# Sums of weight blocks made in DRAM during an earlier stage of the kernel

## The chip, the core and the metric

The kernel runs on one core of one Trainium2 chip. The engines of the core are named as in the profile: PE is TensorE with its matmuls, PEld its loading of weights, DVE is VectorE, ACT is ScalarE, POOL is GpSimd, SP is SyncE, which here only issues DMAs. The metric is the device time of one execution in microseconds. Before the change it is 2234.42 us, the median of 3 runs (2232.87 to 2238.69).

## What is computed

One transformer block in float32, on 512 tokens of width 2048. A normed input goes through one wide projection, and from it come a state-space mixer (SSD) and a sparse attention; their outputs are projected, and a gated feed-forward network follows.

```
u = rmsnorm(h, attn_norm_w)
z, xbc, dt_raw, q, kc, vc, ... = split(u @ w_in)
mixed = concat([ssd_mixer(z, xbc, ...), nsa_mixer(q, kc, vc, ...)])
h = h + mixed @ w_out
v = rmsnorm(h, ffn_norm_w)
h = h + (silu(v @ w_gate) * (v @ w_up)) @ w_down      # 2048 -> 5632 -> 2048
return rmsnorm(h, final_norm_w)
```

## The kernel before

**Precision.** Every float32 operand is split into a high half, a copy rounded to the type fp32r (made on ACT, line 121), and a low half, the difference (made on DVE, line 124). A product of two blocks is three matmuls: high by high, high by low, low by high.

**Order of the stages.** First the SSD part: the projection w_in in units of 128 columns, each of 16 blocks, with the mixer's own work woven in. Then attention and the output projection. Then the feed-forward network, first gate and up in 22 pairs (NP = 22), then down. A small scheduler (class Sched) holds generators for the woven work. Each block of a unit, that is each three matmuls, is one tick; a generator yields the number of ticks until it wants to go on. `ssd_core` (its tiles are `t`, `pf`, `xt` in the profile) and `compress` are such generators. In the SSD part and in attention the framework reorders the instructions of an engine by a timeline that it simulates; in the feed-forward part the order is the written one (`tc.manual_schedule()`, line 1937). A queue of instructions takes its waits in order on every engine.

**The feed-forward products.** They use a scheme of Strassen's kind. A 256 by 256 weight quarter has four blocks 11, 12, 21, 22, and instead of eight products of blocks it needs seven, M1 to M7. Three of the seven use sums: S1 = 21 + 22, S3 = 21 + 11, and on the way M6 takes S2 = 11 + S1, M3 takes S4 = 12 + 11 after 11 has become 11 + S1. (Signs are folded into how the blocks are stored and the tokens combined.) The other factors are seven forms of the tokens.

**Where sums are made before.** `quad` (line 1494) says for a group of n blocks how each operand comes about:

- gate and up pairs 0 to 20: S1 and S3 by DMA. SP loads 21, then POOL issues a DMA that adds 22 or 11 onto it (line 1292, `accum_op`).
- the last pair: S1 is added on POOL in place in SBUF, after loads of 21 and 22 (line 1275, in the profile line 130, the helper `add`).
- visits 0 to 5 of down: S1 and S3 are both added on POOL in SBUF (lines 1286 and 1275). Four loads a visit: 11, 12, 21, 22.
- visits from 6 on: S1 on POOL in place, S3 by a load of 21 and an accumulating DMA of 11.
- S2 and S4 always on DVE, in place, just before the high half is made (`form`, line 1308; line 130 in the profile, `Z<-Z` and the like).

**Visits of down.** The list `VISITS` gives 35 visits (j, n): output columns j (8 of them) by n of the 22 inner blocks; n is 2, 2, 3, 4, 5, 6, 6, 6 in the first eight and 4, 3, 3, 3, 5 in the last five. The first are small because the hidden activations (g_d, in DRAM, 1792 KB for an inner block) come back one by one through ACT's queue (`feed`, line 1742). The rows of H, one per j, are loaded from h_d by ACT's queue (line 1763). When the last visit of a column is through M6, `add_x` (lines 1809 to 1813) combines; after M5 `squares` (line 1774) takes squares on ACT for the last norm.

**Loads and places.** `advance` (line 1267) walks the list `loads` in order. For each entry it finds a free place in SBUF (zones Z, A, E; for down 38 places of 64 KB in Z, 8 in E, 6 in A), issues the load on SP's queue (line 1290), and with `plus` the accumulating DMA on POOL's queue (line 1292); an entry with `both` is added on POOL. Each `Blk` counts its reads and frees its place after the last.

Of the kernel before, what the change touches and what calls it, by code (L numbers as in the profile page):

```python
# [8 lines left out]
F32 = mybir.dt.float32  # L9
F32R = mybir.dt.float32r  # L10
AF = mybir.ActivationFunctionType
ALU = mybir.AluOpType
# [5 lines left out]
NP = NFF // 2  # L18
NJ = KD // 2
# [3 lines left out]
VISITS = [(0, 2), (1, 2), (2, 3), (3, 4), (4, 5), (5, 6), (6, 6), (7, 6), (1, 6), (0, 5), (2, 6), (3, 6), (4, 6), (5, 6),  # L23
          (6, 6), (7, 6), (0, 6), (1, 6), (2, 5), (3, 6), (4, 6), (6, 6), (5, 5), (7, 5), (0, 6), (1, 5), (2, 5), (3, 6),
          (5, 5), (4, 5), (6, 4), (0, 3), (1, 3), (2, 3), (7, 5)]
GRING = 8
G_US, MM_US, AHEAD_US = 7.0, 0.118, 5.0
KSUB = 4
EB = 5
LEAD = 3  # L30
NOA = 2


C_AN, C_FN, C_LN, C_SN, C_CW, C_CB, C_PE, C_W2 = 0, 16, 32, 48, 56, 104, 116, 148
# [9 lines left out]
M1, M2, M3, M4, M5, M6, M7 = range(1, 8)  # L44
# [67 lines left out]
def body(ctx, tc, xT, w_in, w_out, w_gate, w_up, w_down, w1k, w1v, cols, rows, kst, out):  # L112
    nc = tc.nc
    act, dve, pool, pe = nc.scalar, nc.vector, nc.gpsimd, nc.tensor
    sch = Sched()

    def f(ap):
        return ap.bitcast(F32)
# [7 lines left out]
    def mul(eng, o, a, b):  # L126
        eng.tensor_tensor(o, a, b, ALU.mult)  # L127
# [7 lines left out]
    dram = ctx.enter_context(tc.tile_pool(name="dram", bufs=1, space=bass.MemoryType.DRAM))  # L135
    def ps(tag, bufs):
        return psum.tile([128, 512], F32, tag=tag, name="ps_" + tag, bufs=bufs)
# [16 lines left out]
    gy_d = dram.tile([8, 2, 128, 512], F32, name="gy_d")  # L154
    y_d = dram.tile([4, 128, 512], F32, name="y_d")
    at_d = dram.tile([8, 128, 512], F32, name="at_d")
    h1_d = dram.tile([KD, 128, 512], F32, name="h1_d")
    h_d = dram.tile([NJ, 128, 4, 256], F32, name="h_d")
    g_d = dram.tile([NP, 4, 128, 896], F32, name="g_d")
    g8_d = dram.tile([NP // GRING, 7, 128, 512], F32, name="g8_d")  # L160

    pools = {}

    def open_pool(name, stack=None, **kw):
        es = ExitStack()
        pools[name] = (es, es.enter_context(tc.tile_pool(name=name, bufs=1, reuse_waits="tile", **kw)))
        return pools[name][1]
# [60 lines left out]
    def was_read(p):  # L228
        sch.flags.add(("evac", unit_of[id(p)]))
# [401 lines left out]
    def ev_kc(g):  # L631
        def ev(p):
            yield from sch.wait("r1")
            if g == 0:
                sp = pools["kcp"][1]
                R["kc2"] = sp.tile([128, 4, 256], F32, name="kc2")
                R["vc2"] = sp.tile([128, 4, 256], F32, name="vc2")
            for n, b in (("kc2", 0), ("vc2", 64)):
                for par in range(2):
                    mul(dve, R[n][par * 64:par * 64 + 64, g, :], p[b:b + 64, par::2], rrow[b:b + 64, par::2])  # L640
            was_read(p)
            if g == 3:
                sch.flags.add("kc")
        return ev

    def compress():
        yield from sch.wait("kc", "core")
# [529 lines left out]
    def ev_head(c):  # L1177
        def ev(p):
            P2["head", c] = p
            was_read(p)  # L1180
            yield 1
        return ev
# [4 lines left out]

    for c in range(NOA):
        units.append(Unit(w_out[c][:, 8:16, :], 8, ma_rhs, ev_head(c)))
# [191 lines left out]
    def pre_oa():  # L1381
# [29 lines left out]
        sch.add(stat_s())  # L1411
        for c in range(NOA):
            sch.add(head_oa(c))

    def head_oa(c):
        if c > 1:
            yield from sch.wait(("oa", c - 2))
        yield from ev_oa(c)(P2.pop(("head", c)))

    def stat_s():  # L1420
        yield 4
        yield from rms_stats(rrow, D, P2["srow"], "s", keep=True, gap=2)
# [55 lines left out]
    def oa_psum(c):  # L1478
        def get():
            if c >= NOA + 2:  # L1480
                sch.run_until(("oa", c - 2 - NOA))
            p = ps("gstgst"[(c // 2 + 0) % 3], 2)
            return p, p
        return get

    for c in range(KD):
        b = Blk(8, 1, w_out[c][:, 8:16, :])
        b.ghost = c < NOA
        loads.append(b)
        Step(b, lambda k: P2["ma"][k], oa_psum(c),  # L1490
             after=lambda p, c=c: sch.add(ev_oa(c)(p)) if c >= NOA else None)


    def quad(src, lo_, hi_, by_dma=True, s3_by_pool=False):

        n = hi_ - lo_

        def a(i, k):
            return src[i - 1, k - 1][:, lo_:hi_, :]
        if by_dma:  # L1500
            q = {"11": Blk(n, 3, a(1, 1)), "12": Blk(n, 2, a(1, 2)), "S1": Blk(n, 2, a(2, 1), a(2, 2)),
                 "S3": Blk(n, 1, a(2, 1), a(1, 1)), "22": Blk(n, 1, a(2, 2))}
        else:
            q = {"11": Blk(n, 3, a(1, 1)), "12": Blk(n, 2, a(1, 2)), "21": Blk(n, 1, a(2, 1)), 
                 "22": Blk(n, 2, a(2, 2)), "S3": Blk(n, 1, a(2, 1), a(1, 1))}
            if s3_by_pool:
                q["11"].reads, q["21"].reads = 4, 2
                q["S1"] = Blk(n, 2, both=(q["21"], q["22"]))
                q["S3"] = Blk(n, 1, both=(q["21"], q["11"]), inplace=True)
            else:  # L1510
                q["S1"] = Blk(n, 2, both=(q["21"], q["22"]), inplace=True)
        q["form"] = {M1: (q["11"], ()), M2: (q["12"], ()), M6: (q["11"], [(q["11"], q["S1"])]), M7: (q["S3"], ()),
                     M5: (q["S1"], ()), M3: (q["12"], [(q["12"], q["11"])]), M4: (q["22"], ())}
        return q

    def add_loads(q, order="11 S1 12 S3 22"):
        loads.extend(q[a] for a in order.split())
# [19 lines left out]
    def v_rhs(p):  # L1537
        a = V_OF[p]
        if a == 0:
            return lambda k: (P2["V0"][:, k, 0, :], P2["V0"][:, k, 1, :])  # L1540
        if a < 3:
            return lambda k: (P2["VV"][:, a - 1, k, 0, :], P2["VV"][:, a - 1, k, 1, :])
        return lambda k: (P2["T"][a - 3][:, k, 0, :], P2["T"][a - 3][:, k, 1, :])
# [41 lines left out]
    def g_forms(u):  # L1585
# [17 lines left out]
        yield 6  # L1603
        if u % GRING == GRING - 1:
            nc.scalar.dma_start(g8_d[u // GRING].rearrange("v p n -> p v n"), f(sg).rearrange("p v s t -> p v (s t)"))
        else:
# [30 lines left out]
    qs = {}  # L1637
# [9 lines left out]
    for n, (side, p) in enumerate(seq):  # L1647
# [3 lines left out]
        q = qs[0, side]  # L1651
        b, sums = q["form"][p]
        if p in (M3, M6):
            sums = [(q["11"], q["S1"]), (q["12"], q["11"])] if p == M3 else ()
# [3 lines left out]
    for u in range(1, NP - 1):  # L1658
        for side in range(2):
            add_loads(qs[u, side])  # L1660
            af, bk = gu_after(u, side), banks()
            for p in SEQ:
                b, sums = qs[u, side]["form"][p]
# [49 lines left out]
        return get  # L1713

    for side, w in ((0, w_gate), (1, w_up)):
        q = qs[NP - 1, side] = quad(w[NP - 1], 0, 8, by_dma=False)
        q["11"].reads, q["22"].reads = 4, 3
        q["S3"] = Blk(8, 1)
        q["form"][M7] = (q["S3"], [(q["11"], q["22"])])
    for side, a in ((0, "11"), (1, "11"), (0, "21"), (0, "22"), (0, "S1"), (1, "21"), (1, "22"), (1, "S1"),  # L1720
                    (0, "S3"), (1, "S3"), (0, "12"), (1, "12")):
        loads.append(qs[NP - 1, side][a])
    for slot, p in enumerate(SEQ_L):
        bk = pair_bank()
        for side in range(2):
            b, sums = qs[NP - 1, side]["form"][p]
            s = Step(b, v_rhs(p), bk(side), after=last_out(p) if side else None, sums=sums)
        done[slot - GRING] = s.i
    done[-1] = s.i
# [8 lines left out]

    pieces = [(n, a) for n in range(NP) for a in (range(7) if n % GRING == GRING - 1 else (None,))]
    pace = {"at": 0.0, "n": 0}  # L1740

    def feed(i):

        if pace["n"] < len(pieces):
            n, a = pieces[pace["n"]]
            if done.get(n - GRING, i) + 2 <= i and clock[i] >= pace["at"]:
                if n == NP - 1:
# [17 lines left out]
    def g_rhs(p, lo_):  # L1765
        a = V_OF[p]
        return lambda k: (G[lo_ + k][a][:, 0, :], G[lo_ + k][a][:, 1, :])
# [146 lines left out]
        return before  # L1914

    for v, (j, a, b) in enumerate(visits):
        q = quad(w_down[j], a, b, by_dma=False, s3_by_pool=v < 6)
        for x in ("11", "12", "21", "22", "S1", "S3"):
            q[x].down = True
        if v == min(i for i, x in enumerate(visits) if x[2] == NP):  # L1920
            keep = Blk(8, 1)
            keep.down = True
            loads.append(keep)
        add_loads(q, "11 12 21 22 S1 S3")
        end = v == len(visits) - 1
        af, bk = d_end(j) if end else d_after(j, a == 0, b == NP), banks(BANK_D)
        for n, p in enumerate(SEQ_END if end else SEQ_D):
            blk, sums = q["form"][p]
            s = Step(blk, g_rhs(p, a), (lambda: (lambda t: (t, t[:, 0:256]))(bank())) if end else bk(p), after=af(p),
                     before=down_before(v, n) if v < NJ - 1 else None, sums=sums)  # L1930
        done.update((i, s.i) for i in range(a, b))
# [37 lines left out]
    for g in range(4):  # L1969
        for k in range(4 * g, 4 * g + 4):  # L1970
            if k % 4 < 2:
                issue_low(2 * g + k % 4)
            t = xt[:, k, :]
            w = col(C_AN + k)
# [4 lines left out]
    for k in range(KD):  # L1979
        t = xt[:, k, :]  # L1980
# [11 lines left out]
    open_pool("kcp")  # L1992
    open_pool("ssd")
    open_pool("ssdc")
    sch.add(ssd_core())
    sch.add(compress())
    sch.add(attention())
# [113 lines left out]
```

## Time and profile before

| | |
|---|---|
| median of 3 runs | 2234.42 us |
| the profiled execution's own time | 2233.11 us |
| its span, first to last instruction | 2231.3 us |
| mean granted TensorE clock | 0.991 |
| DMA | 419.59 MB, 188 GB/s on the mean |

A busy time is the sum over the instructions of one engine. A row of a stretch has, after the stretch and its length, the busy us of PE, PEld, DVE, ACT and POOL, each with its count of instructions, and then the granted clock (1.00 is full speed), the busy share of the 16 DMA engines, and GB/s. A row of instructions in time order has the start, the duration, engine and line, operation, output and inputs, shape; what stands in square brackets is how long the engine sat idle before it and which engine or DMA ended that. Tiles are named by the program (R holds halves of weights, Z, A and E hold weights, ps_g, ps_s and ps_t are PSUM banks). ACTq and SPq are the issuing queues of ACT and SP. A DMA row ends with the median time from issue to landing.

### The profile page before, as it was taken

To read this page: it belongs to the slowest core of one execution; us is meant where nothing else is said; L and a number is where in the kernel's file an instruction comes from. 1 tells how busy PE (TensorE), PEld (TensorE's weight loads), DVE (VectorE), ACT (ScalarE), POOL (GpSimd) and SP (SyncE) were. 2 spreads that over 40 slices of the span, in tenths; PEclk is the share of its full clock that TensorE was granted. 3 is DMA by queue.
4 is the path that set the end of the run, shared out by engine and by line. 5 is a ranking of instruction groups with operands and counts; after the bars stand their busy time and mean duration, and the time that the engine had idled before them with its cause. 6 is when DMAs were issued, how large, how long until landed. Compare 5 with 4: busy or idle time off the path is not lost.

```text
span 2231.3 us, 39774 instructions
## 1 busy us (share of the span) xinstructions
PE 2174.8 (97%) x15392; PEld 2029.9 (91%) x15392; DVE 1806.5 (81%) x2912; ACT 1090.2 (49%) x1770; POOL 427.6 (19%) x433
## 2 busy tenths in 40 slices
PE   9999999999999899999999999999999899999996
PEld 7888888888888778999999999999999899999995
DVE  6799767788788687887888888888888887778887
ACT  5554457567666544444444444444444343333353
POOL 0012243333133053001000000000001221211132
PEclk9999999999999999999999999999999999999998
DMA  6222443222434176788788887878876967778775
GB/s 202 88 75 66 145 149 105 70 89 83 167 121 148 38 247 176 222 244 233 213 245 227 245 229 216 241 222 254 226 219 224 338 206 260 239 250 258 221 174 146
DMA packets 153646, 419.59 MB, mean 188 GB/s; under 512 B 16512, under 2 KB 24720, under 8 KB 153456
## 3 DMA queue, kind: packets, MB, share of 16 engines
q1 hardware_dynamic: 99712, 252.63, 32.9%
q0 software_dynamic: 25456, 77.37, 18.0%
q10 hardware_dynamic: 28288, 87.04, 11.2%
q8 instruction: 121, 1.98, 0.4%
q14 instruction: 69, 0.57, 0.1%
HBM read 353.54 MB, written 59.51 MB: 185 GB/s over the span
## 4 chain that ended last, share of the span: by engine, by line
PE 83%; DVE 8%; DMA 4%; issue 2%; ACT 1%; POOL 1%; SPq 0%; ACTq 0%; DVEq 0%; POOLq 0%
PE ps_g L258 7%; PE ps_g L257 7%; PE ps_g L259 7%; PE ps_t L1373 6%; PE ps_g L1373 6%; PE ps_t L1371 6%; PE ps_t L1372 6%; PE ps_g L1372 6%; PE ps_g L1371 6%; PE ps_s L1373 6%; PE ps_s L1371 6%; PE ps_s L1372 6%; DVE R L124 2%; PE ps_v L994 2%; PE ps_t L967 1%
## 5 line engine op out<-in xcount | busy, mean ns | idle before, releaser
L121 ACT ACTIVATE R<-Z 128x1024 fp32r<-128x1024 f32 (+5 forms) x477 | 433.4, 926 | 544.4 <-DVE Z L130 314.5
L124 DVE TENSOR_TENSOR R<-Z,R 128x1024 fp32r<-128x1024 f32 (+5 forms) x371 | 391.1, 1059 | 28.2 <-ACT R L121 17.8
L257 PE MATMUL ps_g<-u,whi 128*128 128x512 f32 x736 | 292.5, 398 | 0.7 <-DVE h L127 0.7
L259 PE MATMUL ps_g<-u,wlo 128*128 128x512 f32 x736 | 290.7, 395 | 0.0
L258 PE MATMUL ps_g<-u,whi 128*128 128x512 f32 x736 | 290.0, 394 | 0.2 <-DVE u L124 0.2
L1371 PE MATMUL ps_s<-u,R 128*128 128x256 f32 (+1 forms) x747 | 215.5, 289 | 1.7 <-ACT R L121 1.7
L1372 PE MATMUL ps_s<-u,R 128*128 128x256 f32 (+1 forms) x747 | 214.9, 288 | 0.0
L1371 PE MATMUL ps_g<-u,R 128*128 128x256 f32 (+1 forms) x748 | 213.8, 286 | 0.2 <-ACT R L121 0.2
L1372 PE MATMUL ps_g<-u,R 128*128 128x256 f32 (+1 forms) x748 | 213.2, 285 | 0.0
L1371 PE MATMUL ps_t<-u,R 128*128 128x256 f32 (+1 forms) x705 | 202.6, 287 | 0.2 <-ACT R L121 0.2
L1372 PE MATMUL ps_t<-u,R 128*128 128x256 f32 (+1 forms) x705 | 202.1, 287 | 0.0
L124 DVE TENSOR_TENSOR wlo<-wraw,whi 128x512 fp32r<-128x512 f32 x200 | 156.4, 784 | 50.3 <-ACT whi L121 49.7
L1373 PE MATMUL ps_g<-u,R 128*128 128x256 f32 (+1 forms) x620 | 178.2, 287 | 3.0 <-DVE R L124 2.9
L121 ACT ACTIVATE whi<-wraw 128x512 fp32r<-128x512 f32 x200 | 124.8, 626 | 114.9 <-PE ps_g L258 82.3
L1373 PE MATMUL ps_s<-u,R 128*128 128x256 f32 (+1 forms) x595 | 170.4, 286 | 2.5 <-DVE R L124 2.5
L259 PEld LDWEIGHTS ps_g<-u,wlo 128*128 128x128 f32 x736 | 138.7, 188 | 27.1
L257 PEld LDWEIGHTS ps_g<-u,whi 128*128 128x128 f32 x736 | 138.8, 189 | 26.8 <-ACT pth L121 1.1
L258 PEld LDWEIGHTS ps_g<-u,whi 128*128 128x128 f32 x736 | 138.7, 189 | 26.9 <-DVE u L124 0.5
L1371 PEld LDWEIGHTS ps_s<-u,R 128*128 128x128 f32 x747 | 140.5, 188 | 4.1 <-ACT R L121 2.1
L1372 PEld LDWEIGHTS ps_s<-u,R 128*128 128x128 f32 x747 | 141.0, 189 | 2.2
L1371 PEld LDWEIGHTS ps_g<-u,R 128*128 128x128 f32 x748 | 140.7, 188 | 1.8 <-ACT R L121 0.4
L1372 PEld LDWEIGHTS ps_g<-u,R 128*128 128x128 f32 x748 | 141.0, 189 | 1.5
(469 smaller groups left out, 6420.3 us busy)
## 6 DMA issues: line engine op xcount, KB each, us to landing
Z<-in_w_gate SPq DMA_DIRECT2D x95, 512.0 KB, 5.2
Z<-in_w_up SPq DMA_DIRECT2D x93, 512.0 KB, 7.2
wraw<-in_w_in SPq DMA_DIRECT2D x164, 256.0 KB, 3.1
g_d<-A ACTq DMA_DIRECT2D x22, 1792.0 KB, 7.2
Z<-in_w_down SPq DMA_DIRECT2D x59, 384.0 KB, 5.6
u<-g_d ACTq DMA_DIRECT2D x11, 1792.0 KB, 9.4
Z<-in_w_gate POOLq DMA_DIRECT2D x35, 512.0 KB, 7.5
Z<-in_w_up POOLq DMA_DIRECT2D x35, 512.0 KB, 5.7
```

Source lines behind the costliest of these rows:

```text
L121: act.activation(dst, src, AF.Copy, scale=scale)
L124: eng.tensor_tensor(dst, src, f(hi), ALU.subtract)
L257: pe.matmul(p, hi_t[i][:, j, :], ah, start=(k == 0), stop=False)
L258: pe.matmul(p, hi_t[i][:, j, :], al, start=False, stop=False)
L259: pe.matmul(p, lo_t[i][:, j, :], ah, start=False, stop=(k == u.nk - 1))
L967: pe.transpose(p[:, kb * 128:(kb + 1) * 128], e[:, kb * 128:(kb + 1) * 128], ident)
L994: R["pv"] = pe.matmul(o[:, kb * 128:512], v[:, kb, br, :], rhs, start=False, stop=(br == 1 and kb == 3 and t is tl))
L1371: pe.matmul(q, h[:, k, :], ah, start=(k == 0), stop=False)
L1372: pe.matmul(q, h[:, k, :], al, start=False, stop=False)
L1373: pe.matmul(q, l[:, k, :], ah, start=False, stop=(k == s.blk.n - 1))
```

## The change

The sums are no longer made while the feed-forward part runs, but in DRAM and ahead, by a new generator `weight_sums`, which is added to the scheduler just before `ssd_core`. It has 36 parts. For each it copies the first block group from the weights to a scratch tensor in DRAM, by a DMA from ACT's queue, and three steps later adds the other terms onto it with accumulating DMAs from POOL's queue, one for S1 and S3, two for S2, three for S4. All these DMAs keep their written place on their engines. Six ticks lie between parts, and one more after each accumulation. In all there are 36 copies and 51 accumulations.

Made so are S1 for visits 0 to 7, S3 for visits 0 to 5, all of S1 to S4 for visits 30 to 34, and S1 for gate and up of the last pair. These visits load the finished sums as they load any block. For visits 30 to 34 M6 and M3 take S2 and S4 as they are, with no sum on DVE, and a visit has seven loads. Visits 8 to 29 are as before.

```
+V_S1, V_S3, V_S1_END, V_ALL = 8, 6, 30, 30
...
+def made_sums(v):
+    sums = {}
+    if v < V_S1 or v >= V_S1_END:
+        sums["S1"] = ("21", "22")
+    if v < V_S3 or v >= V_ALL:
+        sums["S3"] = ("21", "11")
+    if v >= V_ALL:
+        sums["S2"] = ("21", "22", "11")
+        sums["S4"] = ("21", "22", "11", "12")
+    return sums
...
+    sum_d = {(v, a): dram.tile([128, n, 128], F32, name=f"{a}_d{v}") for v, (j, n) in enumerate(VISITS)
+             for a in made_sums(v)}
+    sl_d = dram.tile([2, 128, 9, 128], F32, name="sl_d")[:, :, 0:8, :]
...
+    def weight_sums():
+        parts = []
+        at = [0] * NJ
+        for v, (j, n) in enumerate(VISITS):
+            k = slice(at[j], at[j] + n)
+            at[j] += n
+            for a, terms in made_sums(v).items():
+                parts.append((sum_d[v, a], [w_down[j][int(t[0]) - 1, int(t[1]) - 1][:, k, :] for t in terms]))
+        parts += [(sl_d[a], [w[NP - 1][1, 0], w[NP - 1][1, 1]]) for a, w in enumerate((w_gate, w_up))]
+        yield 0
+        for n in range(len(parts) + 3):
+            if n < len(parts):
+                tc.keep_in_program_order(nc.scalar.dma_start(parts[n][0], parts[n][1][0]))
+            yield 6 // 2
+            if n >= 3:
+                o, (_, *terms) = parts[n - 3]
+                for t in terms:
+                    tc.keep_in_program_order(nc.gpsimd.dma_start(o, t, accum_op=ALU.add))
+                    yield 1
+            yield 6 // 2
...
-    def quad(src, lo_, hi_, by_dma=True, s3_by_pool=False):
+    def quad(src, lo_, hi_, by_dma=True, made={}):
...
+        q = {"11": Blk(n, 3, a(1, 1)), "12": Blk(n, 2, a(1, 2)), "22": Blk(n, 1, a(2, 2)),
+             "S3": Blk(n, 1, a(2, 1), a(1, 1))}
+        for x in made:
+            q[x] = Blk(n, 2 if x == "S1" else 1, made[x])
+        if "S1" not in made:
...
+        if "S4" in made:
+            q["form"][M6], q["form"][M3] = (q["S2"], ()), (q["S4"], ())
+            q["11"].reads = q["12"].reads = q["S1"].reads = 1
...
-        q = qs[NP - 1, side] = quad(w[NP - 1], 0, 8, by_dma=False)
-        q["11"].reads, q["22"].reads = 4, 3
+        q = qs[NP - 1, side] = quad(w[NP - 1], 0, 8, made={"S1": sl_d[side]})
+        q["11"].reads, q["22"].reads = 4, 2
...
-    for side, a in ((0, "11"), (1, "11"), (0, "21"), (0, "22"), (0, "S1"), (1, "21"), (1, "22"), (1, "S1"),
+    for side, a in ((0, "11"), (1, "11"), (0, "S1"), (1, "S1"), (0, "22"), (1, "22"),
...
-        q = quad(w_down[j], a, b, by_dma=False, s3_by_pool=v < 6)
+        made = {x: sum_d[v, x] for x in made_sums(v)}
+        q = quad(w_down[j], a, b, by_dma=False, made=made)
...
-        add_loads(q, "11 12 21 22 S1 S3")
+        add_loads(q, "11 12 S2 S4 S3 22 S1" if "S4" in made else "11 12 S1 S3 22" if made else "11 12 21 22 S1 S3")
...
+    sch.add(weight_sums())
     sch.add(ssd_core())
```

More of the change, by code (lines that the diff above doesn't have):

```diff
@@ L1499, in a @@
             return src[i - 1, k - 1][:, lo_:hi_, :]
[L1500 to L1509, printed above, removed]
-            else:
+        q = {"11": Blk(n, 3, a(1, 1)), "12": Blk(n, 2, a(1, 2)), "22": Blk(n, 1, a(2, 2)),
[3 more added lines that the diff above has]
+        if "S1" not in made:
+            if by_dma:
+                q["S1"] = Blk(n, 2, a(2, 1), a(2, 2))
+            else:
+                q["21"] = Blk(n, 1, a(2, 1))
+                q["22"].reads = 2
                 q["S1"] = Blk(n, 2, both=(q["21"], q["22"]), inplace=True)
@@ L1916, in body @@
     for v, (j, a, b) in enumerate(visits):
-        q = quad(w_down[j], a, b, by_dma=False, s3_by_pool=v < 6)
-        for x in ("11", "12", "21", "22", "S1", "S3"):
+        made = {x: sum_d[v, x] for x in made_sums(v)}
+        q = quad(w_down[j], a, b, by_dma=False, made=made)
+        for x in set(q) - {"form"}:
             q[x].down = True
```

## The prediction

> **What bounds the kernel now.** I read the page first, then busy time by stretch, then in the two weak stretches the engines in order of time, and last the waits of the end.
>
> ```profile
> span 2231.3 us, 39774 instructions
> ...
> PE 2174.8 (97%) x15392; PEld 2029.9 (91%) x15392; DVE 1806.5 (81%) x2912; ACT 1090.2 (49%) x1770; POOL 427.6 (19%) x433
> ```
>
> TensorE (PE) is busy all but 56 us, so a change that adds no matmul and removes none can win only where PE pauses. Each row below is a stretch: busy us and instruction counts of PE, PEld, DVE, ACT, POOL, then granted clock, DMA share, GB/s.
>
> ```profile
> 100.00:250.00 150.00, 149.25 (x780) 125.79 (x779) 140.81 (x271) 74.56 (x119) 27.13 (x18) 1.00 0.22 73
> 250.00:315.00 65.00, 65.00 (x344) 55.49 (x343) 47.03 (x98) 35.60 (x74) 21.34 (x35) 1.00 0.61 193
> ...
> 1500.00:1690.00 190.00, 190.00 (x1609) 190.00 (x1608) 158.38 (x178) 86.21 (x97) 15.60 (x18) 1.00 0.80 229
> 1690.00:1740.00 50.00, 48.92 (x411) 48.51 (x411) 43.37 (x46) 20.02 (x24) 10.86 (x6) 1.00 0.68 252
> 1740.00:1770.00 30.00, 21.71 (x148) 19.90 (x147) 24.03 (x50) 11.26 (x28) 4.80 (x5) 0.89 0.83 312
> 1770.00:1800.00 30.00, 29.28 (x241) 28.55 (x240) 28.64 (x41) 11.31 (x19) 8.59 (x4) 1.00 0.87 312
> ...
> 1850.00:1925.00 75.00, 72.33 (x597) 70.62 (x596) 54.95 (x73) 26.00 (x34) 13.55 (x10) 1.00 0.82 262
> ...
> 2150.00:2215.00 65.00, 55.96 (x437) 52.43 (x435) 54.36 (x99) 32.13 (x61) 19.76 (x21) 1.00 0.63 138
> ```
>
> In 1500 to 1690, 1609 matmuls take 190 us: 0.118 us each. By that rate the other stretches lack matmuls: 1690 to 1740 lacks 12 (1.5 us), 1740 to 1770 lacks 106 (12.5 us, part of it because the clock fell to 0.89), 1770 to 1800 lacks 13 (1.5 us), 1850 to 1925 lacks 38 (4.5 us) and 2150 to 2215 lacks 113 (13 us). The change touches all but the fourth: it holds the last gate/up pair and visits 0 to 5 (1690 to 1800) and visits 30 to 34 (2150 to 2215). The work added falls in the first two rows, where PE does not pause and DVE (VectorE) is at 141 of 150 us.
>
> **The first stretch.** PE waits there for DVE, which makes the low halves of the weights:
>
> ```profile
> 1708.19 0.39 PE L1373 MATMUL ps_t<-T,R 128*128 128x256 f32 x1 [0.81 <-DVE R L124]
> ...
> 1758.52 0.58 PE L1373 MATMUL ps_t<-V,R 128*128 128x256 f32 x1 [1.92 <-DVE R L124]
> ```
>
> Why DVE is late stands beside the POOL adds that the change removes. The POOL rows come first, then DVE.
>
> ```profile
> 1693.82 6.33 POOL L130 TENSOR_TENSOR Z<-Z 128x1024 f32<-128x1024 f32 x2 [14.19 <-DMA Z<-in_w_gate]
> 1732.28 2.93 POOL L130 TENSOR_TENSOR Z<-Z 128x256 f32<-128x256 f32 x2 [32.13 <-DVE A L130]
> 1738.23 1.89 POOL L130 TENSOR_TENSOR Z<-Z 128x256 f32<-128x256 f32 x2 [3.03 <-DMA Z<-in_w_down]
> 1753.97 1.32 POOL L130 TENSOR_TENSOR Z<-Z 128x512 f32<-128x512 f32 x1 [7.09 <-DMA Z<-in_w_down]
> ```
> ```profile
> 1697.98 3.24 DVE L130 TENSOR_TENSOR Z<-Z 128x1024 f32<-128x1024 f32 x1
> ...
> 1705.78 1.22 DVE L130 TENSOR_TENSOR Z<-Z 128x1024 f32<-128x1024 f32 x1
> ...
> 1732.84 1.77 DVE L130 TENSOR_TENSOR A<-A,Z 128x1024 f32<-128x1024 f32 x1
> 1734.53 1.75 DVE L124 TENSOR_TENSOR R<-Z,R 128x1024 fp32r<-128x1024 f32 x1
> ...
> 1738.39 1.13 DVE L127 TENSOR_TENSOR A<-A,rrow 128x512 f32<-128x512 f32 x1
> 1739.45 0.96 DVE L124 TENSOR_TENSOR R<-Z,R 128x256 fp32r<-128x256 f32 x1
> ...
> 1740.99 0.42 DVE L124 TENSOR_TENSOR R<-Z,R 128x256 fp32r<-128x256 f32 x1
> ...
> 1743.55 0.69 DVE L127 TENSOR_TENSOR A<-A,rrow 128x512 f32<-128x512 f32 x1
> ...
> 1755.50 2.30 DVE L124 TENSOR_TENSOR A<-A 128x1024 fp32r<-128x1024 f32 x1
> ...
> 1767.77 0.42 DVE L130 TENSOR_TENSOR A<-ps_s,A 128x256 f32<-128x256 f32 x1 [2.09 <-DMA A<-h_d]
> ```
>
> The add at 1697.98 has the shape of the one at 1705.78 and takes 2.02 us more; it ends 1.07 us after POOL's second add. In visits 0 to 3 the excess is 0.55 and 0.53 (1.77 and 1.75 against 1.22), 0.44 (1.13 against 0.69), 0.54 (0.96 against 0.42) and 1.08 (2.30 against 1.22): 3.1 us. The Trainium skill, "SBUF — State Buffer", section "Who interferes with whom", says that GpSimd and a VectorE instruction with two SBUF inputs exclude each other for a whole instruction. The trace agrees: 1697.98 + 3.24 is 1701.22, one plain duration (1.22) after POOL's adds were nearly done. By the rule every DVE sum that starts inside a POOL add waits out its rest, and up to the whole 12 us of the four POOL rows could come back; by the rows it is the 5.1 us of excess.
>
> Gain: without POOL's adds the pair loses its DVE excess of 2.0 us, of which PE can take only what it lacks, 0.8 to 1.5; I take 1.1. The 3.1 us lie where DVE has hardly a pause and PE waits for it: all 3.1 count. Visits 4 and 5 give at most the 1.5 that is missing, say 0.7. Sum 4.9. Upper bound: the 15.5 us that the three rows lack, less what DVE's other work keeps; were the clock to stay up (30 us at 0.89), 3.3 us more than 4.9, so 8.2.
>
> Price: S1 and S3 of visits 0 to 5 are now loaded beside 11, 12 and 22, five blocks where four were: 22 blocks of 64 KB, 1.44 MB, at the 312 GB/s of the rows 4.6 us of DMA time, if no DMA time is free; at least nothing, since PE and DVE rarely wait for weights here. DMA share is 0.68 to 0.87, and at 1767.77 DVE does wait 2.09 us for a transfer. I take 1.0. Net 3.9 (0.3 to 8.2). Visits 6 and 7 lose a POOL add each, where PE lacks nothing: nothing. Their S3 and all of visits 8 to 29 stay as they are. The new order of loads costs nothing: the last pair has eight loads as before, now S1 where 21 was, and DVE's lag covers them; without it, one block set of 0.5 MB is 1.7 us at 312 GB/s.
>
> **The end.**
>
> ```profile
> ACT R L121 <- DVE Z L130: 24.7, 9, 5.0
> ```
> ```profile
> 2162.56 0.69 DVE L1813 TENSOR_TENSOR A<-A 128x512 f32<-128x512 f32 x1
> ...
> 2173.53 0.68 DVE L1813 TENSOR_TENSOR A<-A 128x512 f32<-128x512 f32 x1
> ...
> 2177.72 0.56 DVE L130 TENSOR_TENSOR Z<-Z 128x384 f32<-128x384 f32 x1
> ...
> 2183.60 0.69 DVE L1813 TENSOR_TENSOR A<-A 128x512 f32<-128x512 f32 x1
> ...
> 2193.67 0.69 DVE L1813 TENSOR_TENSOR A<-A 128x512 f32<-128x512 f32 x1
> ...
> 2205.59 0.68 DVE L1813 TENSOR_TENSOR Z<-Z 128x512 f32<-128x512 f32 x1
> ```
>
> L1813 runs once in each of these visits, after product M6, and so marks their period. Between the five marks lie 75, 63, 63 and 81 matmuls, 8.9, 7.4, 7.4 and 9.6 us at 0.118; the marks are 10.97, 10.07, 10.07 and 11.92 us apart. Lost: 2.1, 2.7, 2.7, 2.3, together 9.8; the remaining 3 are before the first and after the last mark. The wait row says through what: ACT, which makes the high halves, waits 24.7 us for DVE's sums (11+S1, 12+11). With S2 and S4 loaded, both sums (0.56 each at n = 3, by the row at 2177.72) and that wait go. Next late is DVE itself, with its low halves and output adds. At the least a period loses the two sums, 1.1 us for each of four periods, 4.4; at the most all 9.8. I take 6.5, nearer the lower, because the squares of the finished rows stay on ACT. Two more loads and no accumulating DMA per visit cost nothing while the DMA share is 0.63; without that cover, the two extra loads of 18 blocks in all, 36 blocks or 2.4 MB, take 7.6 us at 312 GB/s, and the gain would be gone.
>
> **The SSD part.** Added are 36 DRAM copies from ACT's queue and 51 accumulating DMAs from POOL's, 342 blocks or 22.4 MB.
>
> ```profile
> L1607 ACTq DMA_DIRECT2D g_d<-A x20: 366/367/393, 913.5 to 1757.8; - x20
> ```
> ```profile
> L1292 POOL DMA_DIRECT2D Z<-in_w_gate x35 | 30.4, 869 | 255.7 <-DMA Z<-in_w_gate 243.3 <-issue 7.1 <-DVE rst L127 5.3
> ```
> ```profile
> u<-g_d ACTq DMA_DIRECT2D x11, 1792.0 KB, 9.4
> ...
> Z<-in_w_down POOLq DMA_DIRECT2D x11, 384.0 KB, 5.0
> ...
> h_d<-A POOLq DMA_DIRECT2D x16, 256.0 KB, 2.7
> ```
> ```profile
> 203.07 3.16 POOL L127 TENSOR_TENSOR t<-xt,rowc 128x512 f32<-128x512 f32 x1 [5.89 <-DVE xt L130]
> ```
> ```profile
> 210.38 0.42 DVE L130 TENSOR_TENSOR t<-ps_t,t 128x256 f32<-128x256 f32 x1
> ```
>
> ACT issues in 0.37 us: 36 are 13 us, on an engine half idle there. POOL issues in 0.87 us: 51 are 44 us, on an engine busy 27 of 150. The DMA share of 0.22 at 73 GB/s leaves room. New are waits: S2 is two accumulations and S4 three into the same DRAM tile, so 15 of them must wait on POOL until the one before has landed, less a step of three matmuls (0.6 us, from 780 in 150). No row shows an accumulation into DRAM. The nearest accumulates into SBUF and lands in 5.0 us; a plain store into DRAM lands in 2.7, and the slowest large transfer in 9.4. That makes 31 to 132 us of waiting, with 5.0 as the likeliest: 4.4 each, 66 us. Behind each wait POOL's queue holds the SSD products (t, pf), the sums of y, the stores of y, and the loads of the compression weights. DVE waits for t: here it had 210.38 - 206.23, 4.2 us to spare. One wait of 4.4 us is just covered; the two in a row of an S4, 9.7 us with an issue, are not. Five of these over 150 us meet some 2 or 3 of the 8 t products and cost each perhaps 2 us, and DVE has 9 us free. So 0 to 5 on PE; I take 2.
>
> **Sum.** 2233.1 us is the profiled execution's time (span 2231.3 and 1.8 around it). 3.9 + 6.5 - 2 = 8.4 off gives 2224.7. The median of the runs, 2234.4, is 1.3 above it: forecast 2226.0 us.
>
> **Rivals.** (1) POOL's waits bind the SSD part. For it: DVE is busy 141 of 150 us there, a queue takes its waits in order, and at 9.4 us a landing the waits would fill 132 of the 123 us that POOL has free. Against: t is ready 4.2 us early, and the sums can run into the next stretch. If half of the 66 us reaches DVE, 33 less the 9 free, PE loses 24: 2234.4 + 24 - 10.4 = 2248. The gain is gone from a loss of 10.4 us; from 17.1 the kernel is slower. The Trainium skill, "DMA: Bandwidth & Descriptors", section "Anatomy of one DMA — SWDGE (gpsimd) path", says that a semaphore wait happens on the issuing sequencer, not in the DMA engines; no run shown so far has such a chain. Chance 0.15. (2) The extra loads bind the first visits, and the transition gives nothing: 2234.4 - 6.5 + 2 = 2229.9. For it stands the DMA share of 0.83 to 0.87, against it that PE waits there for DVE. 0.14. (3) The end is bound by ACT's squares or by the seven loads of a visit, and gives nothing: 2234.4 - 3.9 + 2 = 2232.5. For it: DVE is busy only 54 of 65 us there, so something else holds part of the period; against it the wait row. 0.10. (4) Both upper bounds and an unharmed SSD part: 2234.4 - 8.2 - 9.8 = 2216.4. 0.06. The forecast keeps 0.55.
>
> **Numbers.** What a measurement of this kernel can tell from no change is 0.3%, 6.7 us: faster is below 2227.7, slower above 2241.1. The forecast's own range is 2220 to 2229, with its bounds, nine tenths of it below 2227.7. Faster: 0.50 of it and (4), 0.56. Same: its other 0.05, (2) and (3), 0.29. Slower: (1), 0.15. A range from 2217 to 2239 leaves out (1) and most of (4).
>
> **What would show it.** Right: POOL has no add before visit 8; the 3.24 and 2.30 of DVE become 1.22; 1740 to 1770 gains 30 or more matmuls; the marks of L1813 stand 9 us or less apart. Wrong: DVE rows before 315 us that wait for POOL's t or pf, PE under 780 matmuls in 100 to 250, or PE waiting for loads of S2 and S4.

## The result and the profile after

The changed kernel takes 2245.86 us (median of 6 runs, 2243.81 to 2249.81); before, timed beside it, takes 2234.16. The ratio is 1.0051, with a 95% interval of 1.0041 to 1.0061: slower by some 11 us, where 2226.0 was forecast. The profiled execution took 2245.6 us, again 1.8 around its span.

From here on line numbers are those of the kernel they belong to; in the changed kernel L146 is the helper `add`, L140 makes low halves, L137 high halves, L682 issues the accumulations, L699 the compression's weights, L1855 is `add_x`. First the page after, span and busy times:

```profile
span 2243.8 us, 39888 instructions
...
PE 2180.2 (97%) x15392; PEld 2033.6 (91%) x15392; DVE 1788.2 (80%) x2902; ACT 1092.4 (49%) x1772; POOL 429.5 (19%) x458
```

PE has the same number of matmuls, and DVE has 18 us less. Next, marks at the borders of the stages: per line the instruction, how often, shortest, median and longest in ns, and the start of the first and of the last one. Before:

```profile
L913 POOL MEMSET vz<- x1: 549/549/549, 311.3 to 311.3; 128x512 f32 x1
L1371 PE MATMUL ps_s<-u,R x747: 277/281/498, 780.7 to 2206.2; 128*128 128x256 f32 x175, 128*128 128x512 f32 x12
L1796 ACT ACTIVATE A<-ps_t x3: 364/366/367, 1745.3 to 1814.8; 128x256 f32<-128x256 f32 x3
```

After:

```profile
L953 POOL MEMSET vz<- x1: 542/542/542, 333.0 to 333.0; 128x512 f32 x1
L1411 PE MATMUL ps_s<-u,R x747: 277/281/498, 802.1 to 2220.4; 128*128 128x256 f32 x175, 128*128 128x512 f32 x12
L1838 ACT ACTIVATE A<-ps_t x3: 362/363/365, 1768.7 to 1834.2; 128x256 f32<-128x256 f32 x3
```

And `add_x` after, in order of time:

```profile
2170.02 0.69 DVE L1855 TENSOR_TENSOR A<-A 128x512 f32<-128x512 f32 x1
2181.39 0.69 DVE L1855 TENSOR_TENSOR A<-A 128x512 f32<-128x512 f32 x1
2191.09 0.68 DVE L1855 TENSOR_TENSOR A<-A 128x512 f32<-128x512 f32 x1
2199.91 0.69 DVE L1855 TENSOR_TENSOR A<-A 128x512 f32<-128x512 f32 x1
2208.72 0.69 DVE L1855 TENSOR_TENSOR A<-A 128x512 f32<-128x512 f32 x1
2218.29 0.68 DVE L1855 TENSOR_TENSOR Z<-Z 128x512 f32<-128x512 f32 x1
```

The zeroing of vz stands at the end of the SSD part, ps_s<-u,R opens the feed-forward part, A<-ps_t is M1 of visits 0, 3 and 6, and the rows of `add_x` are visits 29 to 34. The account by marks:

| mark | before | after | later by |
|---|---|---|---|
| vz, end of the SSD part | 311.3 | 333.0 | 21.7 |
| feed-forward part begins | 780.7 | 802.1 | 21.4 |
| M1 of the last pair | 1710.8 | 1730.9 | 20.1 |
| M1 of visit 0 | 1745.3 | 1768.7 | 23.4 |
| M1 of visit 6 | 1814.8 | 1834.2 | 19.4 |
| visit 29 | 2151.2 | 2170.0 | 18.8 |
| visit 34 | 2205.6 | 2218.3 | 12.7 |
| end of the span | 2231.3 | 2243.8 | 12.5 |

The feed-forward part gives 8.9 us, 6.1 of it at the end; the SSD part costs 21.7, not 2. By stretch, after:

```profile
100.00:250.00 150.00, 146.03 (x759) 121.83 (x759) 142.28 (x267) 74.01 (x117) 55.40 (x55) 1.00 0.76 171
250.00:315.00 65.00, 54.67 (x254) 44.68 (x253) 33.73 (x66) 27.19 (x51) 25.88 (x35) 0.89 0.77 192
...
2165.00:2230.00 65.00, 59.70 (x489) 58.03 (x487) 52.74 (x102) 37.51 (x70) 12.28 (x15) 0.99 0.67 169
```

The first two rows had 780 and 344 matmuls and a DMA share of 0.22 and 0.61. Now 21 and 90 are missing, and the share is 0.76 and 0.77. So most of the loss falls in the second row, which the prediction's sum did not price. There the granted clock is 0.89, where it was 1.00, so a part of the 90 may be the slower clock and not the wait itself. Who waits there, in the order of POOL and time (in brackets the idle time before, and what ended it; the last row is PE):

```profile
239.29 0.81 POOL L682 DMA_DIRECT2D S_d<-in_w_down  x1 [5.08 <-DMA S_d<-in_w_down]
...
248.63 0.81 POOL L682 DMA_DIRECT2D S_d<-in_w_down  x1 [5.00 <-DMA S_d<-in_w_down]
254.95 0.81 POOL L682 DMA_DIRECT2D S_d<-in_w_down  x1 [5.50 <-DMA S_d<-in_w_down]
255.49 1.55 POOL L146 TENSOR_TENSOR xt<-xt,t 128x512 f32<-128x512 f32 x1
...
290.75 0.88 POOL L682 DMA_DIRECT2D S_d<-in_w_down  x1 [7.48 <-DMA S_d<-in_w_down]
291.32 1.44 POOL L699 DMA_DIRECT2D w1r<-in_w1k  x2
...
257.09 0.69 PE L594 MATMUL ps_t<-ident,xt 128*128 128x128 f32 x2 [4.65 <-POOL xt L146]
```

A chain of accumulations holds POOL 5 to 7.5 us at a time, and behind it stand the sums of y (xt) and the loads of the compression's weights (w1r). PE waits for both: the last row shows the first, and these waits between 220 and 330 us (total, times, longest) the second:

```profile
ACT w1h L137 <- DMA w1r<-in_w1k: 16.4, 6, 5.8
...
PEld ps_s L717 <- ACT w1h L137: 8.4, 4, 4.4
```

No row shows DVE waiting for t or pf of POOL, the path that the prediction priced. The rule cited there from the Trainium skill, "DMA: Bandwidth & Descriptors", section "Anatomy of one DMA — SWDGE (gpsimd) path", that the wait is on the issuing sequencer, agrees with POOL's row at 290.75: idle for 7.48 us, with the next load of w1r issued right behind it. The DMA queues in the first 800 us (packets, MB, share of 16 engines' time; q0 is POOL's, q10 ACT's) before and after:

```profile
q0 software_dynamic: 6336, 16.42, 5.9%
```
```profile
q0 software_dynamic: 13520, 28.87, 16.3%
q10 hardware_dynamic: 5184, 9.44, 3.9%
```

On q0 this is 12.45 MB and 10.4% of 800 us more, 83 us of all sixteen engines. (The accumulations are 198 blocks, 12.98 MB; the row of before holds some 0.5 MB of its feed-forward part, which begins 21 us earlier.) That makes some 6.5 us for a MB; the copies' 9.44 MB took 31 us, 3.3 for a MB.

### The profile page after: what moved, and what is told of

It reads as the page before. It is cut to its first block, busy times and chain, and to the rows that moved or that the text cites. A ratio compares the mean times of both kernels' runs of the same rounds, so it can differ in the third digit from the quotient of the medians.

```text
span 2243.8 us, 39888 instructions
## 1 busy us (share of the span) xinstructions
PE 2180.2 (97%) x15392; PEld 2033.6 (91%) x15392; DVE 1788.2 (80%) x2902; ACT 1092.4 (49%) x1772; POOL 429.5 (19%) x458
## 4 chain that ended last, share of the span: by engine, by line
PE 81%; DVE 6%; DMA 6%; issue 4%; POOL 2%; ACT 1%; SPq 0%; DVEq 0%; ACTq 0%; POOLq 0%
PE ps_g L278 6%; PE ps_g L277 6%; PE ps_g L276 6%; PE ps_t L1413 6%; PE ps_s L1413 6%; PE ps_t L1411 6%; PE ps_g L1413 6%; PE ps_s L1411 6%; PE ps_t L1412 6%; PE ps_s L1412 6%; PE ps_g L1412 6%; PE ps_g L1411 6%; DMA Z<-in_w_down 2%; PE ps_v L1034 2%; PE ps_t L1007 1%
## 5 line engine op out<-in xcount | busy, mean ns | idle before, releaser
L137 ACT ACTIVATE R<-Z 128x1024 fp32r<-128x1024 f32 (+5 forms) x471 | 430.2, 932 | 535.2 <-DVE Z L146 294.7
L140 DVE TENSOR_TENSOR R<-Z,R 128x1024 fp32r<-128x1024 f32 (+5 forms) x365 | 374.2, 1032 | 29.1 <-ACT R L137 20.4
L140 DVE TENSOR_TENSOR wlo<-wraw,whi 128x512 fp32r<-128x512 f32 x200 | 159.2, 804 | 53.1 <-ACT whi L137 52.3
L137 ACT ACTIVATE whi<-wraw 128x512 fp32r<-128x512 f32 x200 | 124.6, 626 | 119.6 <-PE ps_g L277 86.0
```

What stands on the lines that cost most here:

```text
L137: act.activation(dst, src, AF.Copy, scale=scale)
L140: eng.tensor_tensor(dst, src, f(hi), ALU.subtract)
```

## The experiments

Two theories. **Queue:** what POOL has to do waits behind accumulations that wait for each other. **Bytes:** the added traffic itself delays the loads of the SSD part, whoever issues it. "Place" is a part of the second: beside the attention the DMA engines are about as busy in before (share 0.31 from 311 to 780 us) as in the SSD part (0.34 from 20 to 311), but the stage is longer, and the added bytes are spread (with the sums 0.56 in f1's attention, 0.70 in the SSD part of the changed kernel). Each run was compared with before on the same chip; "us" is the ratio's distance from 1 times 2234.4, "cost" is that less the -8.7 of the run without accumulations, which has the whole gain and only the copies. The intervals reach 2 to 3 us to each side, so the difference of two costs is good to some 3 us.

| run | where, how | ratio (95%) | us | cost | feed-forward from | it lasts |
|---|---|---|---|---|---|---|
| before | | 1 | 0 | | 780.7 | 1450.6 |
| the change | SSD part, chained | 1.0051 (1.0041 to 1.0061) | +11.4 | 20.1 | 802.1 | 1441.7 |
| e1 | attention, chained | 1.0022 (1.0012 to 1.0032) | +4.9 | 13.6 | 793.2 | 1442.0 |
| e2 | SSD part, unchained | 1.0013 (1.0004 to 1.0023) | +2.9 | 11.6 | 796.4 | 1442.6 |
| e3 | SSD part, copies for accumulations | 0.9986 (0.9976 to 0.9995) | -3.1 | 5.6 | 787.1 | 1442.0 |
| e4 | SSD part, no accumulations | 0.9961 (0.9949 to 0.9974) | -8.7 | 0 | 782.1 | 1441.0 |
| f1 | attention, unchained | 0.9979 (0.9969 to 0.9990) | -4.7 | 4.0 | 788.0 | 1441.5 |
| f2 | attention, sums of sums | 0.9965 (0.9953 to 0.9978) | -7.8 | 0.9 | 782.2 | 1442.3 |
| f3 | SSD part, two copies for each | 1.0027 (1.0015 to 1.0038) | +6.0 | 14.7 | 790.3 | 1444.8 |
| f4 | SSD part, a sixteenth of the bytes | 0.9966 (0.9956 to 0.9975) | -7.6 | 1.1 | 781.7 | 1442.4 |
| g1 | f2, h loaded by POOL | 0.9945 (0.9931 to 0.9959) | -12.3 | -3.6 | 785.7 | 1439.5 |
| g2 | f2, without visits 0 to 7 | 1.0036 (1.0023 to 1.0049) | +8.0 | | 782.0 | 1458.3 |
| g3 | SSD part, sums of sums | 1.0025 (1.0015 to 1.0035) | +5.6 | 14.3 | 793.3 | 1445.1 |
| h1 | the change, w1r loaded by SP | 1.0019 (1.0008 to 1.0030) | +4.2 | 12.9 | 793.8 | 1443.0 |

The two right columns are from the one profiled execution of each, which can be some us off the median (g1's took 2227.0, its median is 2220.5). All runs with the sums gain 7.6 to 11.1 us in the feed-forward part, but f3 (5.8), g3 (5.5) and g2; the first two were not followed further.

**e1: beside the attention**

```
-        yield 0
+        yield from sch.wait("cmp")
```

> The sums start only when the compression is through, so that they run beside attention; all else is the changed kernel, 2245.9 us. Queue theory (POOL's waits for its own accumulations delay the sums of y and the loads of the compression weights, and that is the 21.4 us that the first feed-forward matmul is late): those two have gone before, so nearly all of the 21.4 us comes back, 2225 to 2230, the rest for attention's own POOL work that now stands behind the waits. Traffic theory (22.4 MB more through the DMA engines cost the time wherever they run): attention's DMA share is as low as the SSD part's, so 2240 or more. Order theory (more instructions make the simulated timeline place the SSD work worse): between the two, unforeseeable.

2240.71 us. The mark of vz was back at 311.3, but the attention lost 12.5. Place is part of it, not all: chained accumulations hold POOL there too (60.1 us of waits from 311 to 800 us).

**e2: the terms of one sum four parts apart**

```
-                for t in terms:
-                    tc.keep_in_program_order(nc.gpsimd.dma_start(o, t, accum_op=ALU.add))
+            for k in range(3):
+                p = n - 3 - 4 * k
+                if 0 <= p < len(parts) and k + 1 < len(parts[p][1]):
+                    tc.keep_in_program_order(nc.gpsimd.dma_start(parts[p][0], parts[p][1][k + 1], accum_op=ALU.add))
```

> The same 36 copies and 51 accumulations in the same stretch, but the second term of a sum is issued four parts after the first and the third four after that, so that hardly any accumulation waits for the one before it. Queue theory: the 103 us that POOL waited at this line fall below 20, and most of the 21.4 us comes back, 2225 to 2232. Issue theory (the 51 issues of 0.82 us themselves, 42 us of POOL, are the delay) and traffic theory: no change, 2243 to 2249.

2237.77 us, between the two expectations. POOL's wait for accumulations from 110 to 340 us, in the changed kernel and then here (ahead of 110 us, where PE loses nothing, both have some 52 more):

```profile
POOL S_d L682 <- DMA S_d<-in_w_down: 45.9, 12, 7.5
```
```profile
POOL S_d L682 <- DMA S_d<-in_w_down: 5.5, 5, 1.9
```

40 us of waits are gone, and 8.5 us of cost with them; 11.6 stay. In e2 the loads of w1r from in_w1k still land in 7.0 us (4.5 in before), and between 220 and 330 us ACT waits 22.2 us for w1r, where before has 3.0:

```profile
ACT w1h L137 <- DMA w1r<-in_w1v: 12.0, 6, 5.9
...
ACT w1h L137 <- DMA w1r<-in_w1k: 10.2, 6, 3.6
```

**e3: copies in place of the accumulations; e4: neither**

```
-                    tc.keep_in_program_order(nc.gpsimd.dma_start(o, t, accum_op=ALU.add))
+                    tc.keep_in_program_order(nc.scalar.dma_start(junk_d[n - 3][k][:, 0:t.shape[1], :], t))
```

> Each of the 51 accumulations is replaced by a plain copy of the same blocks into other DRAM scratch, from ACT's queue; POOL has none, and the sums are left out (the scratch that is read has the first term alone). Traffic of about the same bytes, no POOL. Queue and issue theories: the SSD part is as before, 2225 to 2229. Traffic theory: 2240 or more.

> The 51 accumulations are left out, so that the sums that are read are the first term alone; the 36 copies from ACT's queue stay. It gives what the feed-forward part gains by itself. By the marks of the two profiles that is 8.9 us: 2225.3 if the copies cost nothing (queue, issue and traffic theories alike), more by what the copies cost. With the run before it, the difference is what the accumulations' traffic costs.

2232.27 and 2226.43 us. e4 is 8.7 us faster than before, where the forecast's two gains add up to 10.4: the gain of the feed-forward part is real, and 36 copies cost about nothing (its feed-forward part begins 1.4 us later). e3 loses 5.6 with no accumulation at all, so copies on another queue cost too; that fits neither expectation's number.

**f3: two copies for each accumulation**

```
+                    for i in (k, k + 3):
+                        tc.keep_in_program_order(nc.scalar.dma_start(junk_d[n - 3][i][:, 0:t.shape[1], :], t))
```

> In the SSD part: each accumulation replaced by two plain copies on ACT's queue to scratch that nothing reads (with one copy: zeroing of vz at 317.2 us, 2232.3 us; with unchained accumulations 325.1 and 2237.8). Computation: the sums stay their first block. An accumulation took the DMA engines about twice a copy's time for each byte (10.4% of 16 engines in the first 800 us for 12.4 MB, against 5.1% for 13 MB), so two copies are its traffic without POOL. Theory that the accumulations' traffic makes the difference between 2232 and 2238: mark at 322 to 326, 2236 to 2239 us. Rival (POOL's issue and waits make it): mark at 317 to 319, 2232 to 2234 us.

2240.12 us, the mark at 323.0: the mark that the expectation's theory named, and a time just above its range. ACT's queue now has the DMA time that copies and accumulations had together:

```profile
q10 hardware_dynamic: 19424, 35.40, 14.3%
```

14.3% here, 3.9 + 10.4 in the changed kernel. With no accumulation on POOL, this costs 14.7 us: the loads of w_in land in 4.6 us between 20 and 340 us, in before in 3.0. Not all of the 14.7 is the bytes' delay of other loads. The feed-forward part lasts 3.8 us longer than e4's, and ACT, which issues these copies, waits 8.3 us for them in that stretch, a queue effect of its own. The Trainium skill, "DMA: Bandwidth & Descriptors", section "Issuing engines are not separate DMA queues", says that transfers started by different engines run on the same 16 DMA engines. The runs agree: a queue of its own did not keep these bytes apart.

**f4: small accumulations, chained**

```
-                    tc.keep_in_program_order(nc.gpsimd.dma_start(o, t, accum_op=ALU.add))
+                    tc.keep_in_program_order(nc.gpsimd.dma_start(o[0:8], t[0:8], accum_op=ALU.add))
```

> In the SSD part, chained as in the changed kernel, but each accumulation moves 8 of the 128 partitions, a sixteenth of the bytes. Computation: the sums are whole only in those 8 partitions. What is left is POOL's issue (51 of 0.8 us) and the fixed time from issue to landing. Theory that POOL's share comes from the time a large accumulation takes to land: waits fall from 100 us to under 60, mark at 314 to 319, 2227 to 2232 us. Rival (issuing and the mere order on POOL cost it): mark at 322 to 330, 2236 to 2243 us.

2227.67 us. Its wait row from 110 to 340 us:

```profile
POOL S_d L682 <- DMA S_d<-in_w_down: 18.6, 9, 3.2
```

The chain, the order on POOL and as many issues are all there, and the cost is 1.1 us. So neither the issues nor the mere order are the price, and more instructions alone (the order theory of e1's expectation) are not either. The waits are shorter, since a small transfer lands sooner, but not by as much as expected (70 us with the start, not under 60); the bytes make both the traffic and the length of the waits.

**h1: the changed kernel, with the compression's weights loaded by SP**

```
-                nc.gpsimd.dma_start(wr, cw[n][:, 2 * c4:2 * c4 + 2, :])
+                nc.sync.dma_start(wr, cw[n][:, 2 * c4:2 * c4 + 2, :])
```

> The changed kernel as it is (sums in the SSD part, chained, 2245.9 us), but the 16 loads of the compression's weights (w1r) are issued by SP instead of POOL, where they stand behind the accumulations' waits. In the changed kernel the first of them was issued 8.2 us later than before (268.6 against 260.4) and the last 21.6 us later (331.5 against 309.9), so 13.4 us were lost while they ran. Theory that these loads are who suffers from POOL's waits: the zeroing of vz comes at 319 to 326 us instead of 333.0, and the time is 2234 to 2240 us. Rival (others on POOL, the sums of y, acc and the stores of gated y, or the bytes alone hold the stretch): mark at 329 to 334, 2242 to 2247 us.

2238.69 us: 7.2 come back, about what e2 brought. The loads of w1r, of the changed kernel and then of h1:

```profile
L699 POOL DMA_DIRECT2D w1r<-in_w1k x8: 574/878/927, 268.6 to 302.9; - x8
L699 POOL DMA_DIRECT2D w1r<-in_w1v x8: 546/550/583, 309.8 to 331.5; - x8
```
```profile
L699 SPq DMA_DIRECT2D w1r<-in_w1k x8: 327/328/1471, 268.1 to 298.3; - x8
L699 SPq DMA_DIRECT2D w1r<-in_w1v x8: 327/328/328, 303.5 to 323.7; - x8
```

The last is issued 7.8 us earlier. Who suffers from POOL's waits is thus mostly this row of loads, one behind another through two buffers; PE still waits 3.9 us for POOL's sums of y (xt). The first still starts 8 us later than before (260.4), which is what was lost ahead of it. The mark of vz, 313.1 in this run, tells nothing here, as POOL reaches it without the loads.

**f1 and f2: both edits, and sums of sums.** f1 is e1 and e2 together. In f2 S2 starts as a copy of S1 and S4 as a copy of S2, so that 36 accumulations of 144 blocks (instead of 198) are enough and no sum has two; the parts are put in another order, so that a sum is made some parts before it is copied:

```
+        for a, b in (("S4", "S2"), ("S2", "S1")):
+            for i, (v, x) in enumerate(made):
+                if x == a:
+                    parts[i] = (sum_d[v, a], [sum_d[v, b], parts[i][1][-1]])
```

> Both earlier edits at once: the sums run beside the attention and the terms of one sum are issued four sums apart. Theory (three costs that add up: POOL's waits for the term before, DMA engine time, and the place in the SSD part): the waits are gone and the place has DMA engines at 0.2 to 0.5 of their time, so the feed-forward part keeps its 9 us and the attention loses 1 to 4: 2227 to 2230 us, and the SSD part's last mark (the zeroing of vz, 311.3 us before and 333.0 after) stays at 311 to 312. Rival (the bytes cost the same wherever they are moved): the attention still loses 8 or more of the 12 us it lost with the chained sums: 2234 to 2238.

> Beside the attention; the three-block and four-block sums of the last five visits start as copies of the two-block and three-block sums, so that there are 36 accumulating transfers instead of 51 and every sum has one. Theory of three costs: no wait for a term before, 30% fewer accumulations: 2226 to 2229 us. Rival (bytes cost the same wherever they are moved): 36/51 of the 12 us lost in the attention is 8.5, so about 2234.

2231.30 and 2226.39 us. With the first runs this is a table of two by two: chained, 20.1 in the SSD part and 13.6 in the attention; unchained, 11.6 and 4.0. The chain costs 8 to 10 in either place, the place 6.5 to 8 with either order. f2 has nearly nothing left to pay (0.9); its fewer bytes and its missing chain were not separated.

**g3: f2's sums back in the SSD part**

> The same 36 accumulations, one for each sum, but in the SSD part again instead of beside the attention. Theory that the SSD part pays for the bytes: 36 accumulations there leave the mark (zeroing of vz, 311.0 us in the one beside the attention) at 317 to 322 and the time at 2231 to 2236. Rival (the chain of several terms was all of it): mark at 311 to 313, 2225 to 2228 us.

2239.21 us, more than expected, although 15 of the 51 accumulations are gone and the mark, 319.6, lies as forecast. Place matters here too; but the run has waits of its own, since a copy of a sum must wait on ACT for an accumulation to land, and POOL's next accumulation for that copy. They show in rows such as these, POOL's first:

```profile
POOL t L143 <- DMA S_d<-S_d: 8.5, 1, 8.5
...
ACT ph L137 <- DMA S_d<-in_w_down: 4.4, 1, 4.4
```

How much of its 14.3 is these waits and how much the bytes was not separated.

**g1: h loaded by POOL.** In the changed kernel visit 0 is 3 to 4 us late against the marks on either side of it (23.4 against 20.1 and 19.4). ACT's rows there, and the weight load that the chain of waits names:

```profile
1755.55 0.40 ACT L137 ACTIVATE R<-Z 128x256 fp32r<-128x256 f32 x1
1762.30 2.07 ACTq L1805 DMA_DIRECT2D A<-h_d  x2
1764.41 0.42 ACT L137 ACTIVATE R<-Z 128x256 fp32r<-128x256 f32 x1 [8.47 <-DMA Z<-in_w_down]
```
```profile
1753.18 9.02 DMA Z<-in_w_down
1762.30 7.21 DMA A<-h_d
```

The conversion at 1764.41 starts 0.04 us after the second issue of h has ended; its own block, the second load of visit 0, was issued at 1739.88 and had landed in 8.7 us. It stood behind h's loads in ACT's queue, and these went 0.1 us after the load of 1753.18 had landed.

```
-        nc.scalar.dma_start(P2["H"][j][:, 1:5, :], h_d[j])
+        nc.gpsimd.dma_start(P2["H"][j][:, 1:5, :], h_d[j])
```

> The sums of sums beside the attention (2226.4 us), and the loads of h for the first visits are issued by POOL, which is idle there, instead of ACT. Theory of the transition's missing 2 us: the issue of h's load stood on ACT from 1755.95 until a weight load issued at 1753.18 had landed at 1762.20, and the conversion of visit 0's second block, whose own data were there, stood behind it in ACT's queue. With the issue on POOL the conversion starts 4 to 7 us earlier: 2222 to 2224.5 us, and the wait of 8.47 us on ACT goes to under 4. Rival: the DMA engines are full there (share 1.04 from 1760 to 1770), so h or the sums land as late as before: 2226 to 2227.5 us, and DVE waits for A<-h_d instead.

2220.51 us, the best of all. POOL and ACT in g1, then the same loads in f2:

```profile
1743.26 1.09 POOL L1812 DMA_DIRECT2D A<-h_d  x2 [56.44 <-issue]
...
1741.02 0.71 ACT L137 ACTIVATE R<-Z 128x256 fp32r<-128x256 f32 x2
...
1750.27 0.42 ACT L137 ACTIVATE R<-Z 128x256 fp32r<-128x256 f32 x1 [4.36 <-DVE Z L146]
```
```profile
1743.14 2.07 ACTq L1812 DMA_DIRECT2D A<-h_d  x2
1745.26 0.42 ACT L137 ACTIVATE R<-Z 128x256 fp32r<-128x256 f32 x1 [8.46 <-DMA Z<-in_w_down]
```

The wait of 8.46 is gone from ACT: both conversions follow each other at 1741.02, and a later one waits 4.36 for DVE instead. The times must be read against a mark, since M1 of the last pair is at 1716.5 in g1 and at 1711.8 in f2. From it, the second conversion starts 8.6 us earlier, h itself leaves 4.6 us earlier, and M1 of visit 0 comes 3.3 us earlier (34.4 after it, 37.7 in f2, 34.5 in before). The feed-forward part is 2.8 us shorter. Why h's loads wait for that weight load stays open.

**g2: visits 0 to 7 as before the change**

> The sums of sums beside the attention, for the last five visits and the last gate/up pair alone: visits 0 to 7 load four blocks and POOL makes their sums, as before the change (14 copies and 14 accumulating transfers fewer). Against 2226.4 us. Theory from the marks of the changed kernel (visit 0 loses 3.25 us, visits 1 to 7 gain 3.95): the first eight visits' sums are worth 0.7 us, so 2226.5 to 2228. Rival, the prediction's step (3.9 us in the transition, of which the pair gave 1.3): they are worth 2.6 us or more, so 2229 to 2231.

2242.22 us, far off both. The loss is at the other end: near 2120 us SP stands still. Its issues there:

```profile
2114.52 0.33 SPq L1337 DMA_DIRECT2D A<-in_w_down  x1
2124.94 12.29 SPq L1337 DMA_DIRECT2D Z<-in_w_down  x6
```

10 us without a load, and PE had 257 matmuls between 2100 and 2140 against 339 in f2. With POOL's sums back in visits 0 to 5 the places in SBUF are handed out in another order, which may have left none free; that was not tried. So the run's time says nothing on the first visits. The marks up to visit 6 do: from M1 of the last pair to M1 of visit 0 it took 36.0 us, f2 37.7, and from there to M1 of visit 6 70.8 us (1747.5 to 1818.3), f2 65.6 (1749.5 to 1815.1). Together f2 is 3.5 us shorter there than g2, the rival's size. But before itself, with the same sums in these visits, took 104.0 against f2's 103.3, which is the theory's 0.7; g2 is slower there than before for a reason that was not found. So what the first visits' sums are worth stays open between the two.

## Why the prediction was wrong, step by step

**The SSD part** is the step that failed: "So 0 to 5 on PE; I take 2". It was 21.4. Two things went wrong. "The DMA share of 0.22 at 73 GB/s leaves room" took the mean of a stretch for a price of nothing; the bytes are worth some 12: e2, with hardly a wait left, keeps 11.6, and f4, with the chain but a sixteenth of the bytes, 1.1. (h1 keeps 12.9 with some of POOL's waits still in it, f3 has 14.7 with waits of ACT's own, so these two are upper figures.) And behind POOL's waits the prediction named t, pf, the sums of y and the compression's loads, but priced t alone. t was not late. The compression's loads were, and POOL's waits, mostly through them, make up the other 7 to 8.5 (h1, e2). No run has both edits in the SSD part, so that the two parts simply add up is not shown. The waits themselves were 45.9 us where POOL has other work, within the bounds of 31 to 132 and under the 66 taken; the accumulations of down landed in a median of 4.6 to 7.9 us by size (128 to 384 KB), most of them above the 5.0 taken.

**Rival 1** had the right sign and nearly the time, 2248, but in part by luck: POOL's waits did cost, yet no DVE row waited for t, and they made less than half of the loss.

**The transition** was forecast at 3.9 and gave 2.0 (21.4 to 19.4). Its mechanism was right: POOL has no add before 1852.9, behind M1 of visit 7, and a DVE add of 1024 columns is back at one plain duration:

```profile
1718.63 1.23 DVE L146 TENSOR_TENSOR Z<-Z 128x1024 f32<-128x1024 f32 x1
```

The term of the wrong size is the price of the loads, "I take 1.0": M1 of visit 0 lost 3.3 against the last pair's. It came through ACT's queue, by h's issue that waited for a weight load, and g1 takes all 3.3 back. Whether that weight load was late for bandwidth is not shown; it took 9.0 us to land.

**The end** was forecast at 6.5 and gave 6.1. The periods went from 10.97, 10.07, 10.07, 11.92 to 9.70, 8.82, 8.81 and 9.57, and ACT's wait for DVE's sums went from 24.7 us to this:

```profile
ACT R L137 <- DVE Z L146: 4.5, 1, 4.5
```

**The signs.** Of those named beforehand, PE under 780 matmuls in 100 to 250 (759) pointed at the fault. The stretch 1740 to 1770, which was to gain 30 matmuls, has 143 against 148 when it is taken 20 us later, at a clock of 0.83. Marks "9 us or less apart" held for two of four.

## What to carry to other kernels

Work moved ahead into a stage must be priced by that stage's own loads: count the DMA engines' time for the added bytes, and list every transfer that stands in the queues it passes, not the one that comes to mind first. Where a chain of dependent DMAs is needed, put other work between the links, build long sums from short ones, and place them where DMA engines have room for long: here the last two together turned 20 us of cost into 1. A DMA's issue that may wait should not stand in the queue of an engine that others wait for.

## What was not expected of the hardware

An accumulating DMA from DRAM into DRAM kept the DMA engines busy for some 6.5 us a MB, twice a plain DRAM copy's 3.3 (3.2 in f3: 25.96 MB in 10.4% of 800 us). And the same 51, chained on POOL, cost 1.1 us with 8 to 32 KB each (medians of 2.4 to 4.9 us to land) and 20.1 us at full size (128 to 512 KB, 4.6 to 9.0 us).
